# Splitting the weights of one projection three pieces ahead instead of two, in a two-layer decoder trunk

## The chip, the cores and the metric

The kernel runs on one core of one Trainium2 chip. The metric is the device time of one execution in microseconds (us). Three executions of the kernel before took 1278.33, 1278.75 and 1279.27 us, a median of 1278.75 us. The engines are named as in the profile: PE (matrix multiplication), DVE (vector), ACT (scalar), POOL, and SP, which issues the weight transfers.

## The reference

Two decoder layers over an input of 512 tokens and 1024 features, in float32. Layer 0 mixes the tokens by a gated linear recurrence, layer 1 by RWKV-7; each is followed by a gated convolutional MLP. The part that matters here is the beginning of the RWKV-7 block:

```python
xs_rkv = jnp.stack([h + xx * mix[0], h + xx * mix[1], h + xx * mix[2]])
rkv = jnp.einsum('sbtd,sde->sbte', xs_rkv, w_rkv)
r, k, v = rkv[0], rkv[1], rkv[2]
...
decay = jnp.exp(-jnp.exp(w))
...
kk = kk / jnp.maximum(jnp.linalg.norm(kk, axis=-1, keepdims=True), 1e-12)
kf = kf * (1.0 + (a - 1.0) * k_a)
...
y = _rwkv7_scan(rh, hs(decay), kh, vh, -kk, kk * ah)
```

So three products of 512x1024 by 1024x1024 (r, k, v), a normalisation of k for each head, and a recurrence over the tokens with 16 heads of 64 features. The kernel does the recurrence in chunks of 64 tokens, and needs for each chunk and head the inverse of a unit triangular matrix.

## The kernel before, in words

**Products in three matmuls.** A float32 product is made of reduced-precision ones. Each factor is split into a high part and the rest: a weight piece `raw` (128 x 1024 numbers, 512 KB) becomes `wh` by a cast on ACT (L94) and `wl` by a subtraction on DVE (L97); `mm3` (L54) then issues wh·xh, wh·xl and wl·xh. The inputs are split in the same way into pairs named `mix` or `early`, also by L94 and L97, from a tile `mt` (the token mix of one block of 128 features: L965 or L967, then L970 on DVE).

**Weight pieces.** All weights of the kernel are one list of pieces in order of use. `next_weights` asks for the piece in use: it issues the loads up to three pieces ahead and the splits up to `ahead` pieces, counted from this one and including it. Loads go through SP's queue. Raw, split and other tiles of this size share one ring of buffers.

**Projection.** `project` computes 512 output features of one of the products: four pieces of two feature blocks each (c = 0 to 3), of which the last two are used together, and four accumulators `acc`. Between its steps it calls `background`, which lets other work go on: generators in lane 0 (`rate`) and lane 1 (`rate1`), and `after`, which makes the inputs of a later product.

**Around the change.** The k product comes first, then r as two projections (features 0 to 511, then 512 to 1023), then v. In this document the pieces of the first projection of r are called pieces 1 to 4 and those of the second 5 to 8. Beside the first projection run `prepare(1)` (L1175 to L1218: decays, the norms of k, and the factors AR and BK of the recurrence for the heads 8 to 15) and `solve(0)` (L1264 on: the triangular inverses for the heads 0 to 7). `solve(0)` makes its matrices on PE (aab, L1287), copies them on ACT into D and O (L1292, L1295, L1296, in two batches of ten copies), turns D on DVE (L1300, 1.95 us in the trace), then takes 31 steps of a product and an addition on DVE, each step needing the one before (D, L1308 and X, L1310), and turns the result twice (LT, L1313 and XN, L1315). PE uses XN at L1334 (m1p). Beside the second projection, `trail(2, mv, ...)` makes the inputs `mix` of v. After v the chunk loop (pe, W, tr, tu, py and others) goes through the recurrence.

**Order.** The order of an engine's instructions is fixed when the program is built: a scheduler takes the instructions as written, with its own estimate of times, and places each engine's. At run time each engine goes through its list in that order, and an instruction that waits holds all that stand behind it on its engine.

Of the kernel before, what the change touches and what calls it, by code (L numbers as in the profile page):

```python
# [44 lines left out]
class Kernel:  # L45
# [944 lines left out]
    @staticmethod  # L990
    def bytok(t):
        return t.rearrange("p (c q t) -> p c q t", q=2, t=C)
# [135 lines left out]
    def rwkv_krv(self, pool, mk, mr, AR, BK, PC, selk, LTs):  # L1128
# [95 lines left out]
        def ev_r(b, ps):  # L1224
            self.need(("r", b))
            rr = self.outer(AR, b)
            nc.vector.tensor_tensor(rr, bytok(ps), rr, ALU.mult)

        def trail(i, out, counts):
            gen = self.mixes(i, out)  # L1230
            return lambda c: [next(gen, None) for _ in range(counts[c])]
# [3 lines left out]
        self.project(mk, lambda o, ps: nc.scalar.copy(self.outer(BK, 4 + o), bytok(ps)), after=trail(0, mr, (0, 0, 2, 2)), rate=1.2, ahead=3)  # L1235
        self.push(prepare(1))
        self.push(self.solve(0, AR, BK, LTs), 1)
        self.project(mr, lambda o, ps: ev_r(o, ps), rate=0.4, rate1=1.2)
        self.project(mr, lambda o, ps: ev_r(4 + o, ps), after=trail(2, mv, (4, 2, 2, 2)), rate=1.3, rate1=0.9)
        self.tasks[0].extend(self.tasks[1])  # L1240
        self.tasks[1].clear()
# [545 lines left out]
```

## Time and profile before

| | us |
|---|---|
| median of three runs | 1278.75 |
| profiled execution, its own time | 1279.1 |
| span of its instructions | 1277.3 |
| PE busy | 1256.0 (98%) |
| DVE busy | 929.2 (73%) |
| ACT busy | 642.8 (50%) |
| POOL busy | 131.1 (10%) |
| mean granted clock of TensorE | 0.998 |

The profiled execution is 0.35 us above the median. Its span leaves out 1.8 us around the first and last instruction. Times in the timelines are counted from the start of the span; a row has its start, its duration, the engine, the line, the operation with its output and inputs, the count of instructions drawn together, and in brackets the idle time just before it with what ended it. Durations overlap with the next instruction's, since the engines are pipelined: a PE matmul of 512 columns lasts 0.39 us in the trace, and the next starts 0.23 us later.

### The profile page before, as it was taken

The page shows a single profiled execution, that of the slowest core. Times are in us where ns is not written, and L with a number is a line of the kernel's source. Part 1 is how long each engine was busy: PE and PEld are TensorE (multiplying, and loading weights), DVE is VectorE, ACT ScalarE, POOL GpSimd, SP SyncE. Part 2 cuts the span into 40 slices and gives each one's busy share as a digit, 9 for nine tenths or more (in the row PEclk, how much of TensorE's full clock was granted, in tenths as well). Part 3 has the DMA queues.
Part 4 walks back from the last instruction along what each step waited for, and adds up shares of the span by engine and source line. Part 5 has one row for each costly group of instructions (what it writes and reads, how often), then busy time and mean ns, then how long its engine had stood idle before and what let it go on. Part 6 is the DMA issues. An engine that isn't in the chain of part 4 may idle for free. (4 is left out here: it accounts for less than half of the span.)

```text
span 1277.3 us, 22409 instructions
## 1 busy us (share of the span) xinstructions
PE 1256.0 (98%) x9259; PEld 1067.4 (84%) x9259; DVE 929.2 (73%) x1412; ACT 642.8 (50%) x1006; POOL 131.1 (10%) x206
## 2 busy tenths in 40 slices
PE   9999999999999999999999898999999999999998
PEld 8777888989898989877778797778889898989896
DVE  5998678767676767789999967778776666666654
ACT  6797455434343434559845356545644334343442
POOL 3000001010101010010012145310010101000000
PEclk9999999999999999999999999999999999999999
DMA  7312335445454544413222122122345454545431
GB/s 228 109 53 97 98 119 114 158 106 167 97 175 89 181 83 137 141 57 110 67 75 68 35 63 85 50 94 83 127 88 181 83 182 83 182 83 182 98 133 66
DMA packets 117829, 141.37 MB, mean 111 GB/s; under 512 B 10138, under 2 KB 91748, under 8 KB 117600
## 3 DMA queue, kind: packets, MB, share of 16 engines
q1 hardware_dynamic: 100528, 122.44, 29.9%
q0 software_dynamic: 16624, 16.47, 8.3%
q8 instruction: 72, 1.18, 0.4%
q10 hardware_dynamic: 576, 1.05, 0.2%
q14 instruction: 29, 0.24, 0.1%
HBM read 135.41 MB, written 4.52 MB: 110 GB/s over the span
## 5 line engine op out<-in xcount | busy, mean ns | idle before, releaser
L97 DVE TENSOR_TENSOR wl<-raw,wh 128x1024 fp32r<-128x1024 f32 (+1 forms) x161 | 194.4, 1213 | 123.6 <-ACT wh L94 103.8
L94 ACT CAST wh<-raw 128x1024 fp32r<-128x1024 f32 (+1 forms) x161 | 165.9, 1043 | 179.8 <-PE acc L54 40.7
L54 PE MATMUL accU<-xs,wh 128*128 128x512 f32 x448 | 138.6, 391 | 0.0
L54 PE MATMUL accG<-xs,wh 128*128 128x512 f32 x448 | 138.6, 390 | 0.0
L54 PE MATMUL acc<-hid,wh 128*128 128x512 f32 x384 | 117.9, 389 | 0.0
L748 DVE TENSOR_TENSOR lo<-raw,hi 128x1024 fp32r<-128x1024 f32 x70 | 85.5, 1222 | 39.4 <-PE accU L54 32.0
L747 ACT CAST hi<-raw 128x1024 fp32r<-128x1024 f32 x70 | 73.7, 1054 | 60.4 <-PE accU L54 25.3
L54 PEld LDWEIGHTS accU<-xs,wh 128*128 128x128 f32 x448 | 83.7, 188 | 17.1
L54 PEld LDWEIGHTS accG<-xs,wh 128*128 128x128 f32 x448 | 83.7, 188 | 17.0
L54 PE MATMUL accU<-xs,wl 128*128 128x512 f32 x224 | 87.2, 389 | 0.0
L54 PE MATMUL accG<-xs,wl 128*128 128x512 f32 x224 | 87.2, 389 | 0.0
L54 PE MATMUL accA<-xt,hi 128*128 128x256 f32 x480 | 83.5, 277 | 0.0
L54 PEld LDWEIGHTS acc<-hid,wh 128*128 128x128 f32 x384 | 71.4, 188 | 14.3
L54 PE MATMUL acc<-xs,wh 128*128 128x512 f32 x256 | 80.9, 398 | 0.0
L694 DVE SCALAR_TENSOR_TENSOR cv<-gpad,pv,cv 128x512 f32<-128x512 f32 x96 | 69.1, 747 | 13.1 <-ACT cv L692 12.7
L848 PE MATMUL acc<-wh,hid 128*128 128x512 f32 (+1 forms) x200 | 76.2, 381 | 0.0
L849 PE MATMUL acc<-wl,hid 128*128 128x512 f32 (+1 forms) x200 | 76.1, 381 | 0.0
L847 PE MATMUL acc<-wh,hid 128*128 128x512 f32 (+1 forms) x200 | 76.1, 381 | 0.0
L54 PE MATMUL acc<-hid,wl 128*128 128x512 f32 x192 | 74.3, 389 | 0.0
L168 POOL DMA_DIRECT2D raw<-in_ffn_w_up_dram x20 | 25.7, 1285 | 469.8 <-DVE x L863 166.5
L54 PEld LDWEIGHTS accA<-xt,hi 128*128 128x128 f32 x480 | 72.6, 188 | 0.0
L54 PE MATMUL accA<-xt,lo 128*128 128x256 f32 x240 | 66.3, 276 | 0.0
(411 smaller groups left out, 2938.0 us busy)
## 6 DMA issues: line engine op xcount, KB each, us to landing
raw<-in_ffn_w_up_dram SPq DMA_DIRECT2D x106, 512.0 KB, 3.9
raw<-in_ffn_w_down_dram SPq DMA_DIRECT2D x48, 512.0 KB, 4.0
raw<-in_ffn_w_up_dram POOLq DMA_DIRECT2D x30, 512.0 KB, 5.7
raw<-in_rwkv_w_rkv_dram SPq DMA_DIRECT2D x24, 512.0 KB, 3.8
raw<-in_lru_w_in_dram SPq DMA_DIRECT2D x16, 512.0 KB, 4.0
raw<-in_lru_w_out_dram SPq DMA_DIRECT2D x8, 512.0 KB, 3.8
raw<-in_rwkv_w_out_dram SPq DMA_DIRECT2D x8, 512.0 KB, 3.8
xd<-x SPq DMA_DIRECT2D x8, 256.0 KB, 2.1
```

The lines of the kernel that those rows point to most:

```text
L54: mm = lambda *a, **kw: self.nc.tensor.matmul(ps, *a, skip_group_check=more, **kw)
L94: put = (self.nc.vector.tensor_copy if dve else self.nc.scalar.copy)(hi, src)
L97: self.nc.vector.tensor_tensor(lo, src, hi.bitcast(F32), ALU.subtract)
L168: self.nc.gpsimd.dma_start(raw, more, accum_op=ALU.add)
L694: nc.vector.scalar_tensor_tensor(cv, pair.gp[:, e, j : j + T], cw(j), cv, ALU.mult, ALU.add)
L747: nc.scalar.copy(hi, f[p])
L748: tt(lo, f[p], hi.bitcast(F32), ALU.subtract)
L847: nc.tensor.matmul(ps, hh[:, s], wh[:, k, m], start=kk == 0, stop=False)
L848: nc.tensor.matmul(ps, hl[:, s], wh[:, k, m], start=False, stop=False)
L849: nc.tensor.matmul(ps, hh[:, s], wl[:, k, m], start=False, stop=kk == blocks - 1)
```

## The change

```diff
-        self.project(mr, lambda o, ps: ev_r(o, ps), rate=0.4, rate1=1.2)
+        self.project(mr, lambda o, ps: ev_r(o, ps), rate=0.4, rate1=1.2, ahead=3)
```

In the first projection of r each split is written one piece earlier: piece 3 in the step of piece 1, piece 4 in that of piece 2, and pieces 5 and 6 with the joined pair. The first step of the second projection has then no split left to write. No instruction is added or taken away, and SP's transfers keep their order; the scheduler places the rest anew.

On ACT the first place is the second batch of copies of `solve(0)`. Ahead of it stands fac (L1177, of `prepare(1)`). The casts `wh_5688` (before) and `wh_5605` (after) are those of piece 4, `wh_5694` (before) is that of piece 5. Before:

```order
L1177 ACTIVATE fac<-BK_4909,oka,pv 128x512
L1292 COPY D_5527<-aab 128x8x32 x2
L1295 COPY D_5527<-aab 32x8x32
L1296 COPY O<-aab 32x8x32
L1295 COPY D_5527<-aab 32x8x32
L1296 COPY O<-aab 32x8x32
L1295 COPY D_5527<-aab 32x8x32
L1296 COPY O<-aab 32x8x32
L1295 COPY D_5527<-aab 32x8x32
L1296 COPY O<-aab 32x8x32
L94 CAST wh_5688<-raw_5599 128x1024
L94 CAST wh_5694<-raw_5686 128x1024
```

and after:

```order
L1292 COPY D_5531<-aab 128x8x32
L94 CAST wh_5605<-raw_5603 128x1024
L1295 COPY D_5531<-aab 32x8x32
L1296 COPY O<-aab 32x8x32
L1295 COPY D_5531<-aab 32x8x32
L1296 COPY O<-aab 32x8x32
L1292 COPY D_5531<-aab 128x8x32
L1177 ACTIVATE fac<-BK_4909,oka,pv 128x512
L1295 COPY D_5531<-aab 32x8x32
L1296 COPY O<-aab 32x8x32
L1295 COPY D_5531<-aab 32x8x32
L1296 COPY O<-aab 32x8x32
```

The cast of piece 4 moved from behind the batch into it, and one fac with it. (The cast of piece 3 moved from behind the first batch to ahead of it.)

On DVE the same place, around the turn of D (L1300) and the first steps of the chain; `wl_5689` (before) and `wl_5606` (after) belong to piece 4, `wl_5695` to piece 5. Before:

```order
L1191 TENSOR_TENSOR AR_4907<-BK_4909,ppad_5259 128x4x128
L1300 STREAM_TRANSPOSE A<-D_5527 128x1024
L97 TENSOR_TENSOR wl_5689<-raw_5599,wh_5688 128x1024
L1308 TENSOR_TENSOR D_5527<-A,X 128x31
L1310 TENSOR_TENSOR X<-X,D_5527 128x31
L1308 TENSOR_TENSOR D_5527<-A,X 128x60
L1310 TENSOR_TENSOR X<-X,D_5527 128x30x2
L1308 TENSOR_TENSOR D_5527<-A,X 128x87
L1310 TENSOR_TENSOR X<-X,D_5527 128x29x3
L1227 TENSOR_TENSOR AR_4906<-acc_5514,AR_4906 128x4x2x64
L1308 TENSOR_TENSOR D_5527<-A,X 128x112
L97 TENSOR_TENSOR wl_5695<-raw_5686,wh_5694 128x1024
```

and after:

```order
L97 TENSOR_TENSOR wl_5606<-raw_5603,wh_5605 128x1024
L1186 TENSOR_TENSOR kp<-BK_4909,pinv 128x512
L1187 SCALAR_TENSOR_TENSOR BK_4909<-BK_4909,pv,kp 128x4x128
L1300 STREAM_TRANSPOSE A<-D_5531 128x1024
L1227 TENSOR_TENSOR AR_4906<-acc_5514,AR_4906 128x4x2x64
L1191 TENSOR_TENSOR AR_4907<-BK_4909,ppad_5259 128x4x128
L1308 TENSOR_TENSOR D_5531<-A,X 128x31
L1310 TENSOR_TENSOR X<-X,D_5531 128x31
L1308 TENSOR_TENSOR D_5531<-A,X 128x60
L1310 TENSOR_TENSOR X<-X,D_5531 128x30x2
L1308 TENSOR_TENSOR D_5531<-A,X 128x87
L1227 TENSOR_TENSOR AR_4906<-acc_5515,AR_4906 128x4x2x64
```

The subtraction of piece 4 moved from behind the turn to ahead of it, and L1191 the other way. Further on the steps of the chain stand more often directly behind each other (12 neighbours of the chain with nothing between them, up to the place shown next, where before had 5).

The second place on DVE is where the last inputs of v and the last piece of r (piece 8, `wl_5955` and `wh_5954` in both) meet. Before:

```order
L1310 TENSOR_TENSOR X<-X,D_5527 128x16x16
L1218 SCALAR_TENSOR_TENSOR AR_4907<-AR_4907,nkk,knb 128x4x128
L1308 TENSOR_TENSOR D_5527<-A,X 128x255
L970 SCALAR_TENSOR_TENSOR mt<-x,pv,mt 128x511
L1310 TENSOR_TENSOR X<-X,D_5527 128x15x17
L1218 SCALAR_TENSOR_TENSOR AR_4907<-AR_4907,nkk,knb 128x4x128
L1308 TENSOR_TENSOR D_5527<-A,X 128x252
L97 TENSOR_TENSOR mix<-mt,mix 128x512
L1310 TENSOR_TENSOR X<-X,D_5527 128x14x18
L97 TENSOR_TENSOR wl_5955<-raw_5874,wh_5954 128x1024
```

and after:

```order
L1310 TENSOR_TENSOR X<-X,D_5531 128x15x17
L97 TENSOR_TENSOR mix<-mt,mix 128x512
L1218 SCALAR_TENSOR_TENSOR AR_4907<-AR_4907,nkk,knb 128x4x128 x2
L1308 TENSOR_TENSOR D_5531<-A,X 128x252
L965 TENSOR_SCALAR mt<-x,om 128x512
L1310 TENSOR_TENSOR X<-X,D_5531 128x14x18
L970 SCALAR_TENSOR_TENSOR mt<-x,pv,mt 128x511
L1218 SCALAR_TENSOR_TENSOR AR_4907<-AR_4907,nkk,knb 128x4x128 x2
L97 TENSOR_TENSOR mix<-mt,mix 128x512
L97 TENSOR_TENSOR wl_5955<-raw_5874,wh_5954 128x1024
```

The L970 whose `mt` is cast just ahead of piece 8 now stands behind three more instructions of the chain: X 15x17, D 252 and X 14x18.

On ACT at that place the cast of piece 8 stands directly behind the cast of that `mt`. Before:

```order
L1210 CAST rec<-rec 40x512
L94 CAST mix<-mt 128x512
L1368 COPY decay<-PC 64x8x8 x4
L94 CAST mix<-mt 128x512
L94 CAST wh_5954<-raw_5874 128x1024
L94 CAST wh_5960<-raw_5952 128x1024
```

and after:

```order
L1210 CAST rec<-rec 40x512
L1368 COPY decay<-PC 64x8x8 x3
L94 CAST mix<-mt 128x512
L1368 COPY decay<-PC 64x8x8
L94 CAST mix<-mt 128x512
L94 CAST wh_5954<-raw_5874 128x1024
L94 CAST wh_5960<-raw_5952 128x1024
```

One cast of `mix` changed places with three small copies; the cast of piece 8 stays behind the second one.

## The prediction

> **What bounds the kernel now.** I read the busy times first, then PE's waits, then the stretch of the change in its timelines.
>
> ```profile
> PE 1256.0 (98%) x9259; PEld 1067.4 (84%) x9259; DVE 929.2 (73%) x1412; ACT 642.8 (50%) x1006; POOL 131.1 (10%) x206
> PEclk9999999999999999999999999999999999999999
> ```
>
> PE is busy for 1256.0 of 1277.3 us, nearly all of it at full clock. The edit leaves every matmul in place, so it can change only PE's waits and its clock. The waits of PE from 640 to 740 us, with total, count and longest:
>
> ```profile
> PE pe L1468 <- DVE tu L1513: 1.8, 2, 1.1
> PE acc L54 <- ACT wh L94: 1.6, 1, 1.6
> PE tr L1438 <- DVE W L1431: 1.5, 1, 1.5
> PE m1p L1334 <- DVE XN L1315: 0.7, 1, 0.7
> ```
>
> The second row is the wait that the edit bears on. In PE's timeline, with the rows to which I return:
>
> ```profile
> 634.36 0.69 PE L1287 MATMUL aab<-AR,BK 64*64 64x64 f32 x32
> ...
> 640.93 1.21 PE L54 MATMUL acc<-mix,wh 128*128 128x512 f32 x4 [1.57 <-ACT wh L94]
> ...
> 670.89 0.39 PE L54 MATMUL acc<-mix,wl 128*128 128x512 f32 x1
> 671.12 2.07 PE L54 MATMUL acc<-mix,wh 128*128 128x512 f32 x8
> ...
> 695.12 1.20 PE L1334 MATMUL m1p<-XN,O 32*32 32x32 f32 x64 [0.75 <-DVE XN L1315]
> ...
> 719.36 0.68 PE L1468 MATMUL pe<-tu,W 128*64 128x64 f32 x14 [1.09 <-DVE tu L1513]
> ```
>
> PE waits 1.57 us for piece 4. Piece 8 (the row at 671.12) starts without a wait. ACT shows why piece 4 is late:
>
> ```profile
> 635.28 0.82 ACT L1177 ACTIVATE fac<-BK,oka,pv 128x512 f32<-128x512 f32 x1 [1.38 <-DVE BK L1192]
> 636.12 0.65 ACT L1292 COPY D<-aab 128x256 f32<-128x256 f32 x2
> ...
> 639.06 0.37 ACT L1295 COPY D<-aab 32x256 f32<-32x256 f32 x1
> 639.45 0.36 ACT L1296 COPY O<-aab 32x256 f32<-32x256 f32 x1
> 639.84 2.95 ACT L94 CAST wh<-raw 128x1024 fp32r<-128x1024 f32 x3
> ...
> 669.45 0.62 ACT L94 CAST mix<-mt 128x512 fp32r<-128x512 f32 x1 [4.26 <-DVE mt L970]
> 669.98 2.00 ACT L94 CAST wh<-raw 128x1024 fp32r<-128x1024 f32 x2
> ```
>
> Its cast begins at 639.84, behind ten copies. The last two rows are the other place: piece 8's cast begins at 669.98 behind a cast of mix that waited 4.26 us for DVE's mt, and ends about 671.0, just as PE arrives. That cover is nearly zero. DVE is the engine with no slack here; the row of windows from 639.4 to 695 us gives PE, PEld, DVE, ACT and POOL busy:
>
> ```profile
> 639.40:695.00 55.60, 53.44 (x418) 43.33 (x418) 54.75 (x114) 25.30 (x50) 7.08 (x18) 1.00 0.23 71
> ```
>
> DVE is busy for 54.75 of 55.60 us. Whatever is put ahead of an instruction there delays it in full.
>
> **The change part by part.**
>
> *The wait for piece 4.* In the new order its cast follows the batch's first copy. The last aab ends at 634.36 + 0.69 = 635.05, a copy takes half of 0.65, a cast a third of 2.95 (0.98): cast done at about 636.4. PE arrives at 640.93 - 1.57 = 639.36. The wait goes: -1.57 on PE. Pieces 5 and 6 follow directly and are wanted only from 650 us, so they cost nothing.
>
> *The turn of D.* The batch took from 636.12 to 639.43 = 3.31, until its last D. Now it can begin at 635.10, but has a cast (0.98) and a fac (0.82, of which 0.72 until the next) inside: 635.10 + 3.31 + 0.98 + 0.72 = 640.11. DVE's rows:
>
> ```profile
> 638.42 0.68 DVE L1191 TENSOR_TENSOR AR<-BK,ppad 128x512 f32<-128x512 f32 x1
> 639.46 1.95 DVE L1300 STREAM_TRANSPOSE A<-D 128x1024 f32<-128x1024 f32 x1 [0.35 <-ACT D L1295]
> 641.35 1.17 DVE L97 TENSOR_TENSOR wl<-raw,wh 128x1024 fp32r<-128x1024 f32 x1
> 642.45 0.19 DVE L1308 TENSOR_TENSOR D<-A,X 128x31 f32<-128x31 f32 x1
> 642.67 0.21 DVE L1310 TENSOR_TENSOR X<-X,D 128x31 f32<-128x31 f32 x1
> ...
> 644.48 0.27 DVE L1308 TENSOR_TENSOR D<-A,X 128x112 f32<-128x112 f32 x1
> 644.66 1.22 DVE L97 TENSOR_TENSOR wl<-raw,wh 128x1024 fp32r<-128x1024 f32 x1
> ...
> 668.68 0.74 DVE L970 SCALAR_TENSOR_TENSOR mt<-x,pv,mt 128x511 f32<-128x511 f32 x1
> 669.34 0.41 DVE L1310 TENSOR_TENSOR X<-X,D 128x255 f32<-128x255 f32 x1
> ...
> 670.33 0.41 DVE L1308 TENSOR_TENSOR D<-A,X 128x252 f32<-128x252 f32 x1
> ```
>
> The turn started at 639.46, 0.03 after its last copy; it will start at about 640.14, so +0.7. DVE itself is there by 639.11 + 1.1 - 0.6 = 639.6 (it takes on a subtraction and gives L1191 away), so ACT sets it.
>
> *DVE up to the last mt before piece 8 (L970 at 668.68).* Start of the turn +0.7; the subtraction of piece 4 leaves, -1.1 (641.35 to 642.45); L1191 comes, +0.6; X 15x17, D 252 and X 14x18 come ahead, about 0.33 each, +1.0. Then the neighbours. D at 642.45 ends at 642.64 and the X that needs it starts at 642.67, 0.03 later; D at 644.48 ends at 644.75 and the independent subtraction starts at 644.66, 0.09 earlier. A dependent neighbour so costs about 0.11 more than an unrelated one, and there are 12 where there were 5: +0.8. Sum 0.7 - 1.1 + 0.6 + 1.0 + 0.8 = +2.0. The transposes rec and knb of `prepare(1)` stand later on PE; at most some 0.4 of waiting for them comes on DVE, the far bound being zero: I take 0.2, so +2.2. Bounds: with no price on neighbours +1.2; with everything late together +2.6.
>
> *The new wait.* The mt, mix, and piece 8's cast hang together on ACT, so the cast and PE's start on piece 8 move from 671.12 to about 673.3. PE would be there at 671.12 - 1.57 = 669.55. So a wait of 3.3 to 3.7 us stands at piece 8, of which 0.4 may already be taken at piece 7, whose subtraction also stands behind more of the chain. PE is 2.2 late where it had been 1.57 early.
>
> *From there to the chunks.* XN's end moves by +0.7 - 1.1 + 0.6 and 8 more dependent neighbours in all (0.9), +1.1, to +1.8 if all small waits add. m1p had 0.75 of wait, so PE's lateness of 2.2 shrinks to max(2.2 - 0.75, 1.1 to 1.8), about 1.7. The masks W and the first tu stand two steps of the chain later: the wait of 1.09 at 719.36 grows by up to 1.4, and the 1.5 at tr, which waits for W, gives most back. I take +0.3 (bounds -0.3 and +0.8). Together +2.0.
>
> *The clock.* This is the largest doubt. The windows show one place in this part where the clock was lowered (the column ahead of the DMA share is the granted clock; PE busy is the second number), and two stretches with waits where it was not:
>
> ```profile
> 793.00:794.00 1.00, 0.33 (x3) 0.20 (x4) 1.00 (x3) 0.69 (x2) 0.43 (x1) 1.00 0.95 393
> 794.00:795.00 1.00, 0.00 (x0) 0.00 (x0) 0.01 (x1) 0.00 (x0) 1.00 (x1) 1.00 0.47 197
> 795.00:796.00 1.00, 0.79 (x27) 0.79 (x28) 0.17 (x1) 0.00 (x0) 0.89 (x3) 1.00 0.08 33
> 796.00:797.00 1.00, 0.41 (x14) 0.31 (x9) 0.99 (x3) 0.69 (x2) 0.40 (x1) 0.91 0.00 0
> 797.00:798.00 1.00, 1.00 (x20) 0.88 (x23) 0.97 (x2) 0.04 (x1) 0.00 (x0) 0.50 0.06 16
> ...
> 800.00:801.00 1.00, 1.00 (x7) 0.91 (x7) 1.00 (x2) 0.26 (x1) 0.00 (x0) 0.88 0.69 110
> ...
> 638.00:642.00 4.00, 2.43 (x12) 1.66 (x11) 3.65 (x5) 3.92 (x8) 0.00 (x0) 1.00 0.46 131
> 730.00:735.00 5.00, 3.50 (x69) 2.53 (x62) 4.79 (x10) 1.60 (x4) 1.38 (x2) 1.00 0.00 0
> ```
>
> In 793 to 797 PE was busy for 1.53 of 4 us; then the clock stood at 0.50 from about 796.8 to 800.2, 3.4 us. At 638 to 642 it was busy for 2.43 of 4 and the clock stayed. A wait of 3.3 us or more at piece 8 leaves 0.7 of 4 us busy, below the closed case; but the stretch that counts may be cut at another point, and a wait split in two halves lies nearer the open case. I hold a closing likelier than not, 2 to 1. At half clock 3.4 us of matmuls do 1.7 us of work, less what of it falls into the wait: 1.1 to 1.7, of which the rest of the wait at m1p takes some 0.1. So about +1.3.
>
> The Trainium skill (TensorE: Matmul & The Clock Gate, Part 1: The HAM clock gate) says that the clock falls to half after at least one idle window of about 3.4 us, on windows that run freely. The length of the slow stretch agrees (3.4 us at 0.50). A gap of 3.3 to 3.7 us seldom fills such a window whole, so by that rule the clock would stay and the sum would be +2.0; the trace speaks against the strict reading, since it closed with 1.53 of 4 us busy.
>
> *Sum.* +2.0 + 1.3 = +3.3 on the profiled execution, 1279.1 to 1282.4; that execution is 0.35 above the median of 1278.75, so about 1282.0 as a median.
>
> **The rivals.** A change under 0.2% (2.6 us) is about what a measurement of this kernel cannot tell from none: from 1276.2 to 1281.3.
>
> *The new wait comes, the clock stays.* For it: two stretches with 30 to 40% idle kept their clock. Against it: the one at 794. Time: 1278.75 + 2.0 = 1280.8, no measurable change. It decides itself by how much of the wait falls into one stretch of about 3.4 us.
>
> *The delay on DVE is mostly absorbed.* If the dependent neighbours cost nothing (-0.8) and the copies of the batch begin early enough for the turn to keep its time (-0.7), mt is late by 0.7 and PE waits about 2.2 at piece 8, for a net of 0.7; m1p's 0.75 takes that, and what is left is -0.3 to +0.8: 1278.5 to 1279.6. This ends on the other side: not slower. The point from which it decides is an mt late by less than about 1.2. Against it: the 0.03 and 0.09 above, and ACT's order.
>
> *The gain stays.* If no new wait appears at piece 8, PE keeps its 1.57: 1277.2. That needs mt no later than before, against +1.0 from the three chain steps alone. Even this is under 0.2%.
>
> **How the numbers follow.** New wait with the slow clock 0.50 (1282.0, its own range 1281.2 to 1283.2), new wait alone 0.25 (1280.8), absorbed 0.17 (1279.0), gain kept 0.08 (1277.2). The predicted time is that of the first, rounded to 1281.9 since the smaller end of the clock's price is as likely as the larger. Slower by over 0.2%: nearly all of the first, with a little of the second, 0.48. Faster: 1277.2 is inside the band, so 0.03 only. The same: 0.49. The range from 1278.9 to 1283.0 leaves out the gain, half of the absorbed case and the far end of the first, about 0.19.
>
> **What the changed profile would show.** PE's row "acc <- ACT wh 1.6" at 641 gone, and a new wait of 3 us or more at the first wh row of piece 8, near 670 to 673 us; the turn L1300 at about 640.1; the last mt near 670.9; m1p's wait below 0.75; the granted clock at 0.50 for 3.4 us near 674 to 677 us. I am wrong if that wait is under 2 us, or if the clock row reads 1.00 there.

## The result, and the profile after

The changed kernel takes 1281.23 us (median of 20 runs, 1280.16 to 1282.74), the kernel before 1278.61 us on the same chip (20 runs, 1277.40 to 1279.87). The ratio is 1.0022, with a 95% interval from 1.0016 to 1.0028: 2.6 us slower. That is just about the 0.2% that I had named as the limit of what can be told from no change, but with 20 runs of each the interval lies clear of 1, so the kernel did become slower. The profiled execution took 1282.44 us (span 1280.4), so it lies 1.2 us above its median. Two of the twelve executions of e6_p4, below, took 1382.30 and 1996.60 us at a mean granted clock of 0.85 and 0.58, and its figures leave these two out.

The page's rows on the engines and the granted clock:

```profile
PE 1258.0 (98%) x9259; PEld 1069.4 (84%) x9259; DVE 930.4 (73%) x1412; ACT 642.7 (50%) x1006; POOL 130.6 (10%) x206
PEclk9999999999999999999998999999999999999999
```

The work is the same, and one slice of the clock now reads 8. PE's waits from 640 to 740 us:

```profile
PE acc L54 <- ACT wh L94: 3.3, 1, 3.3
PE pe L1468 <- DVE tu L1513: 2.9, 2, 2.0
PE acc L54 <- DVE wl L97: 0.8, 1, 0.8
PE tr L1438 <- DVE W L1431: 0.4, 1, 0.4
```

The wait on wh is still one wait, but of 3.3 us instead of 1.6, and the wait of m1p for XN has left the list. PE's timeline says which piece it is:

```profile
617.91 0.60 PE L1208 MATMUL rec<-ident,n 128*40 128x128 f32 x4 [0.49 <-DVE n L1204]
...
663.99 0.50 PE L54 MATMUL acc<-mix,wl 128*128 128x512 f32 x1 [0.75 <-DVE wl L97]
...
670.48 0.40 PE L54 MATMUL acc<-mix,wl 128*128 128x512 f32 x1
674.14 3.78 PE L54 MATMUL acc<-mix,wh 128*128 128x512 f32 x8 [3.27 <-ACT wh L94]
...
699.22 1.20 PE L1334 MATMUL m1p<-XN,O 32*32 32x32 f32 x64
```

The first row serves to set the two traces against each other. In the trace of before it starts at 617.00, and XN, to which I return, at 692.89:

```profile
617.00 0.60 PE L1208 MATMUL rec<-ident,n 128*40 128x128 f32 x4 [0.50 <-DVE n L1204]
```

```profile
692.89 2.08 DVE L1315 STREAM_TRANSPOSE XN<-X 128x1024 f32<-128x1024 f32 x1
```

The row rec stands ahead of everything that the edit moves, so the second trace is 0.91 us late from its start; that has to be taken off each time below. Where I compare the experiments' traces too, I count from this row in each (617.58 in e1, 617.25 in e2, 617.63 in e3, 617.82 in e5, 617.91 in e6, 617.41 in e7, 617.03 in e11, 618.08 in e12). The wait for piece 4 is gone. Piece 8 waits 3.27 us, and its first eight matmuls take 3.78 us where they took 2.07. The windows show why they are slow (PE busy is the second number, the granted clock the one before the DMA share):

```profile
670.00:671.00 1.00, 0.88 (x4) 0.38 (x2) 1.00 (x3) 0.00 (x0) 0.91 (x4) 1.00 0.96 340
671.00:672.00 1.00, 0.00 (x0) 0.00 (x0) 1.00 (x3) 0.00 (x0) 0.86 (x3) 1.00 0.96 291
672.00:673.00 1.00, 0.00 (x0) 0.00 (x0) 1.00 (x2) 0.47 (x1) 0.00 (x0) 0.70 0.61 209
673.00:674.00 1.00, 0.00 (x0) 0.00 (x0) 1.00 (x3) 1.00 (x3) 0.00 (x0) 0.50 0.10 35
...
678.00:679.00 1.00, 1.00 (x3) 0.71 (x3) 0.39 (x1) 0.00 (x0) 0.00 (x0) 0.50 0.42 142
679.00:680.00 1.00, 1.00 (x5) 0.86 (x4) 0.46 (x1) 0.00 (x0) 0.00 (x0) 0.89 0.00 0
```

The clock falls to 0.50 at about 672.4, in the middle of the wait, and comes back at about 679.2: 6.8 us, of which PE spends 5.1 us (674.14 to 679.2) on matmuls at half speed. The median execution probably loses less. The 20 executions have a mean clock from 0.995 to 0.998, with the median between 0.996 and 0.997, and the profiled one is among the four with the lowest. A stretch of 3.4 us at half clock lowers the mean by 1.7 / 1280 = 0.0013, so by this estimate the median execution has about one such stretch fewer; which one is not on record.

ACT and DVE show what came late:

```profile
640.74 0.36 ACT L1295 COPY D<-aab 32x256 f32<-32x256 f32 x1
...
672.52 0.62 ACT L94 CAST mix<-mt 128x512 fp32r<-128x512 f32 x1 [3.81 <-DVE mt L970]
673.05 1.99 ACT L94 CAST wh<-raw 128x1024 fp32r<-128x1024 f32 x2
```

```profile
641.14 2.12 DVE L1300 STREAM_TRANSPOSE A<-D 128x1024 f32<-128x1024 f32 x1 [0.39 <-ACT D L1295]
...
671.72 0.77 DVE L970 SCALAR_TENSOR_TENSOR mt<-x,pv,mt 128x511 f32<-128x511 f32 x1
...
679.54 0.69 DVE L1227 TENSOR_TENSOR AR<-acc,AR 128x512 f32<-128x512 f32 x1 [1.16 <-PE acc L54]
...
696.87 2.14 DVE L1315 STREAM_TRANSPOSE XN<-X 128x1024 f32<-128x1024 f32 x1
```

The turn of D starts when the last D copy ends, the cast of piece 8 stands behind a cast of mix that waited for DVE's mt, and the row at 679.54 is new: DVE itself waits 1.16 us for PE, whose accumulators the slow clock has made late.

### The profile page after: what moved, and what is told of

The parts are those of the page before. It is cut to its first block, busy times and chain, and to the rows that moved or that the text cites. A ratio compares the mean times of both kernels' runs of the same rounds, so it can differ in the third digit from the quotient of the medians.

```text
span 1280.4 us, 22404 instructions
## 1 busy us (share of the span) xinstructions
PE 1258.0 (98%) x9259; PEld 1069.4 (84%) x9259; DVE 930.4 (73%) x1412; ACT 642.7 (50%) x1006; POOL 130.6 (10%) x206
```

## The experiments

All were run in five rounds beside the kernel before. My theory was that the loss has two parts, a late mt that opens a wait at piece 8 and the clock that this wait lowers. The rivals were that the clock costs nothing in the end, and that the cast inside ACT's batch is the whole cause.

**Filling the wait (e1_fill10).** Ten matmuls of a zero weight onto the accumulator; in the trace they stand directly ahead of piece 8. (The tile `zero` and the parameter `fill` are added too.) The scheduler placed a few others anew: ACT's four small copies `decay` now stand behind piece 8's cast, one weight transfer goes out ahead of the transfer `lnw` (L1390) instead of behind it, and the mt of piece 8 starts 53.48 us after rec instead of 53.81.

```diff
-                    for k in range(1 if first else 0, kc):
+                    for k in [self.nc.tensor.matmul(pss[o], self.zero, xs[x0][0], start=False, stop=False) for _ in range(fill if c == n - 1 and o == nob - 1 else 0)][:0] or range(1 if first else 0, kc):
...
-self.project(mr, ..., rate=1.3, rate1=0.9)
+self.project(mr, ..., rate=1.3, rate1=0.9, fill=10)
```

> The changed kernel with ten more matmuls of a zero weight (128x128 by 512 columns, adding zeros to acc) on PE directly ahead of the first matmul of piece 8, where PE waits 3.27 us in the profile of the changed kernel; order on ACT, DVE and POOL as in the changed kernel. They take ten times 0.23 = 2.3 us and should fit into the wait. Theory (part of the loss is the clock, lowered because PE is idle there): the wait at piece 8 shrinks to about 1.0 us, the granted clock reads 1.00 from 660 to 690 us, and the time falls by 0.5 to 1.2 to 1280.0 to 1280.7, about 1.5 to 2.0 above before. Rival (the clock costs nothing in the end, the delay alone makes the loss): 1281.2, as the changed kernel. Rival (PE's throughput after the wait matters, the wait was not free): 1283.5.

Measured: 1279.16 us, 2.1 below the changed kernel, ratio to before 1.0007 (0.9999 to 1.0016). Its timeline, and its row of windows beside that of the changed kernel below it:

```profile
670.39 2.45 PE L214 MATMUL acc<-early,zero 128*128 128x512 f32 x10
673.46 2.14 PE L54 MATMUL acc<-mix,wh 128*128 128x512 f32 x8 [0.62 <-ACT wh L94]
...
697.00 1.20 PE L1334 MATMUL m1p<-XN,O 32*32 32x32 f32 x64 [0.76 <-DVE XN L1315]
```

```profile
640.00:690.00 50.00, 48.62 (x327) 39.05 (x326) 48.98 (x103) 20.77 (x39) 7.76 (x15) 1.00 0.21 68
```

```profile
640.00:690.00 50.00, 45.98 (x277) 36.34 (x276) 47.76 (x97) 18.05 (x31) 5.11 (x15) 0.93 0.20 68
```

PE does 2.3 us more work and the kernel is 2.1 us faster. The clock stays at 1.00, and the eight matmuls of piece 8 take 2.14 us again. The gain is larger than the 0.5 to 1.2 that I expected. Counted from rec, piece 8 starts after 55.88 us, in the changed kernel after 56.23; m1p (697.00) starts after 79.42, in the changed kernel after 81.31. So of the 1.9 us that lie between the two at m1p, 1.5 arise behind the start of piece 8, where the one runs at full clock and the other at half.

One thing stood in the way of that reading. Among PE's waits of the changed kernel, over the whole run, stands

```profile
PE pd L1506 <- issue: 1.4, 1, 1.4
```

and it was gone in this profile, perhaps because ten more instructions stand ahead of it. The 1.9 us stand ahead of that place and can't come from it, but the time of the whole kernel can. So three controls follow.

**The same number of instructions without the work (e11_tiny10).** The ten matmuls at the same place in the changed kernel, 16 columns wide instead of 512.

```diff
-self.nc.tensor.matmul(pss[o], self.zero, xs[x0][0], start=False, stop=False)
+self.nc.tensor.matmul(pss[o][:, 0:16], self.zero, xs[x0][0][:, 0:16], start=False, stop=False)
```

> The ten zero matmuls of the first experiment at the same place in the changed kernel, but 16 columns wide instead of 512: as many instructions on PE, hardly any work (an estimate of 0.05 us each from the 64-column matmuls of the chunk loop), so PE stays idle there. It separates two readings of the first experiment, in whose profile the wait 'issue' of 1.4 us at L1506 near 798 us was gone as well. Theory (the clock): the wait at piece 8 stays near 2.8 us or more, the clock is lowered there in most runs, and the time is 1280.4 to 1281.4, near the changed kernel's. Rival (ten more instructions move the place of the 'issue' wait, and that was the gain): the 'issue' wait gone, 1279.2 to 1279.9.

Measured: 1281.21 us, ratio to before 1.0027 (1.0016 to 1.0039): the changed kernel's time, as expected. The "issue" wait was gone in this profile too, so its absence alone does not give the time of the first experiment.

```profile
669.84 1.18 PE L214 MATMUL acc<-early,zero 128*128 128x16 f32 x10
673.78 3.43 PE L54 MATMUL acc<-mix,wh 128*128 128x512 f32 x8 [2.76 <-ACT wh L94]
```

```profile
669.80:673.20 3.40, 1.22 (x11) 1.08 (x10) 3.15 (x7) 2.01 (x6) 1.79 (x7) 1.00 0.26 37
673.20:676.60 3.40, 2.82 (x7) 2.24 (x8) 3.15 (x6) 0.53 (x1) 3.22 (x7) 0.51 0.96 262
```

PE waits 2.76 us, the clock goes to 0.50 in the next 3.4 us, and the eight matmuls take 3.43 us. So ten matmuls that leave PE idle do not keep the clock up, and ten that fill the wait do. The difference in time, 1281.21 - 1279.16 = 2.05 us, is not the price of the clock alone. Between the two programs stands only the width of ten matmuls, but the scheduler placed other engines' instructions differently:

```profile
671.13 1.01 ACT L1368 COPY decay<-PC 64x64 f32<-64x64 f32 x4 [4.11 <-PE acc L214]
...
677.46 1.05 ACT L94 CAST wh<-raw 128x1024 fp32r<-128x1024 f32 x1 [3.74 <-DMA raw<-in_rwkv_w_rkv_dram]
```

```profile
678.54 1.23 DVE L97 TENSOR_TENSOR wl<-raw,wh 128x1024 fp32r<-128x1024 f32 x1 [1.73 <-ACT wh L94]
```

The four copies wait for the zero matmuls and stand ahead of the casts of mix and of piece 8, so piece 8 starts 56.75 us after rec, 0.87 later than in e1, before any matmul of piece 8 is slow. And DVE waits 1.73 us for a cast whose weight transfer stands behind `lnw` on SP's queue, which went out at 671.16; in e1 one such transfer went out ahead of it, at 662.10. The cleaner figure for the clock is the 1.5 us above.

**The zero matmuls in the kernel before (e5_before_fill10 and e12_before_tiny10).** The same edits with `ahead` left at 2, wide and narrow. The narrow ones stand directly ahead of piece 8 in the trace, the wide ones in three groups from 671.94 to 678.29 among its matmuls.

```diff
-self.project(mr, lambda o, ps: ev_r(o, ps), rate=0.4, rate1=1.2, ahead=3)
+self.project(mr, lambda o, ps: ev_r(o, ps), rate=0.4, rate1=1.2)
```

> Control for the ten zero matmuls: the same ten in the kernel before, at the same place (beside piece 8, where PE does not wait there). Theory (they helped the changed kernel only by keeping PE busy in a long wait): here they cost what the later waits do not take up, 2.3 us less the 0.75 at m1p and some at the chunk loop, so 0.8 to 1.6 above before: 1279.5 to 1280.3. Rival (the matmuls help by themselves, or moved something else): no slower than before, 1278.7 or less.

> The same ten narrow matmuls in the kernel before. Theory (they cost at most 0.5 us of PE, and moving the 'issue' wait is worth little in most runs): 1278.4 to 1279.0. Rival (moving the 'issue' wait is worth 1.0 to 1.9): 1277.0 to 1277.9, faster than before.

Measured: wide 1279.16 us, ratio 1.0002 (0.9994 to 1.0011), less than expected; narrow 1279.72 us, ratio 1.0012 (1.0003 to 1.0021), more than expected. Neither is shown to be faster than before, so nothing says that the ten instructions help by themselves. At m1p PE is 0.82 us later than before in the wide one's profile and 0.97 in the narrow one's, counted from rec; the "issue" wait is gone in both, and what that is worth in the median is open. So is why the narrow ones cost more than the wide ones: they take 1.0 us of PE, not the 0.5 that I had estimated, and the runs spread from 1277.9 to 1282.4.

**The two halves (e2_p34 and e3_p56).** Only pieces 3 and 4, or only 5 and 6, split a step earlier.

```diff
-ws = [self.next_weights(1 if first else ahead) for _ in cs]
+ws = [self.next_weights(1 if first else ahead if isinstance(ahead, int) else ahead[c]) for c in cs]
...
+e2_p34: ahead=[3, 3, 2, 2]
+e3_p56: ahead=[2, 2, 3, 3]
```

> Half of the change: only pieces 3 and 4 split a step earlier, 5 to 8 as before. ACT's second batch of copies has the cast of piece 4 and a fac inside, as in the changed kernel. Theory (the delay of the last mt is made of the late turn of D, +0.7, and of the chain steps and neighbours that the early splits of pieces 5 and 6 bring): the wait for piece 4 (1.6) is gone, a wait of 1.5 to 2 us stands at piece 8, the clock mostly stays, +0.5 to +0.9 on before: 1279.1 to 1279.6. Rival (the cast inside ACT's batch is the whole cause): a wait of 3 us at piece 8 and the full +2.6. Rival (nothing but the early cast of piece 4 matters): -1.6.

> The other half: only pieces 5 and 6 split a step earlier, 3 and 4 as before. Theory: the wait for piece 4 stays at 1.6, a wait of about 1.5 us appears at piece 8, since more steps of the chain stand ahead of its mt, and the time is 1.0 to 1.6 above before: 1279.7 to 1280.3. Rival (the cast inside ACT's batch is the whole cause): no wait at piece 8 and no difference to before. Rival (the two halves do not add): the full +2.6.

Measured: e2 1278.92 us, ratio 1.0003 (0.9994 to 1.0011), a little below what I expected; e3 1279.83 us, ratio 1.0010 (1.0001 to 1.0018), as expected. The waits for wh, first of e2, then of e3:

```profile
671.64 2.14 PE L54 MATMUL acc<-mix,wh 128*128 128x512 f32 x8 [1.74 <-ACT wh L94]
```

```profile
641.55 1.21 PE L54 MATMUL acc<-mix,wh 128*128 128x512 f32 x4 [1.56 <-ACT wh L94]
...
673.02 2.11 PE L54 MATMUL acc<-mix,wh 128*128 128x512 f32 x8 [1.48 <-ACT wh L94]
```

Each half makes its own wait at piece 8, 1.74 and 1.48 us, and the whole change has 3.27 (with 0.75 at piece 7 before it). A wait is not yet a delay, though. Counted from rec, piece 8 starts 0.27 us later than before in e2, 1.27 in e3 and 2.11 in the whole: the wait of e2 is nearly all PE coming earlier, which costs nothing, and that of e3 is nearly all the late mt. The times go with these delays, 0.2 and 1.1 us by the medians. The whole costs 2.6, with 0.6 us more delay than the two halves together and the slow clock besides; in both halves' profiles the eight matmuls of piece 8 take 2.1 us, at full clock. So the cast in ACT's batch is not the whole cause, and two waits at which the clock stayed became one that lowered it.

**Piece 8 ahead of mix (e4_both3_1).** Pieces 7 and 8 also split earlier.

```diff
-self.project(mr, ..., rate=1.3, rate1=0.9)
+self.project(mr, ..., rate=1.3, rate1=0.9, ahead=[2, 3, 3, 3])
```

> The changed kernel with pieces 7 and 8 also split earlier (three ahead from the second step of the second projection of r), so that the cast of piece 8 stands ahead of the cast of mix on ACT. Theory (DVE is full from 640 to 695 us and sets the pace; the place at which PE meets it is secondary): no wait at piece 8, but a wait of about 2 us at the first piece of v for its subtraction on DVE, and m1p waits 1.7; about +1.8 on before, 1280.4, with the clock mostly at 1.00. Rival (the order on ACT behind the late mt is the cause): no wait of over 0.7 us from 650 to 690 us, and 1.6 faster than before, 1277.0.

Measured: 1282.05 us, ratio 1.0033 (1.0021 to 1.0046). PE's waits there:

```profile
678.65 0.39 PE L1258 MATMUL acc<-wl,mix 128*128 128x256 f32 x1 [1.95 <-DVE wl L97]
...
697.03 1.20 PE L1334 MATMUL m1p<-XN,O 32*32 32x32 f32 x64 [1.97 <-DVE XN L1315]
```

```profile
695.00:698.40 3.40, 1.43 (x67) 1.35 (x67) 3.40 (x3) 1.54 (x3) 3.03 (x4) 0.99 0.26 86
698.40:701.80 3.40, 3.40 (x48) 3.18 (x49) 1.45 (x3) 1.15 (x2) 3.15 (x3) 0.50 0.26 73
```

The wait at piece 8 is gone and stands at the next piece, for DVE's subtraction, and at m1p, both as expected. The time was missed by 1.7 us: I had expected the clock to stay, and it fell in this profile after the wait at m1p. That this makes up the 1.7 us is not shown.

**Piece 4 alone (e6_p4).** `ahead=[2, 3, 2, 2]`.

> Only piece 4 split a step earlier; 3, 5, 6, 7 and 8 as before. Theory (removing the wait for piece 4 gains 1.57 at its place, and DVE, full until XN, hands it to a later wait): the wait for piece 4 is gone, rec waits about 1.4 us instead of 0, m1p waits 0.7 to 0.9, and the time is that of before, 1278.5 to 1279.0. Rival (the gain stays when 5 and 6 are left alone): 1277.1.

Measured: 1278.81 us (ten executions), ratio 1.0000 (0.9991 to 1.0009), as expected. The wait for piece 4 is gone, and by the medians nothing is gained:

```profile
PE rec L1208 <- DVE n L1204: 1.1, 1, 1.1
PE m1p L1334 <- DVE XN L1315: 0.7, 1, 0.7
PE sst L1200 <- ACT tmp L1196: 0.3, 1, 0.3
```

rec waits 1.06 and sst 0.32 of the 1.57 us that PE comes earlier. In this profile m1p still starts 0.5 us earlier than before, counted from the first rec; the medians can't tell that from nothing.

**Fewer chain steps ahead of the mt (e7_r2_rate07).** The changed kernel with `rate1=0.7` instead of 0.9 in the second projection.

> The changed kernel with rate1=0.7 instead of 0.9 in the second projection of r, so fewer steps of the chain stand ahead of the last mt before piece 8. Theory (the chain steps ahead of that mt make it late, and the clock goes with the length of the wait): the wait at piece 8 falls from 3.3 to about 2.0 us, the clock is lowered there seldom or for one stretch only, and the time is 0.8 to 1.3 above before: 1279.5 to 1280.0. Rival (ACT's batch and the turn set it): the wait stays at 3 us and the time at 1281.2.

Measured: 1279.71 us, ratio 1.0011 (1.0002 to 1.0019), as expected. The steps of the chain bear on the mt: it starts 52.27 us after rec instead of 53.81, and the wait at piece 8 is shorter:

```profile
672.08 2.11 PE L54 MATMUL acc<-mix,wh 128*128 128x512 f32 x8 [1.85 <-ACT wh L94]
```

The steps that are put off come later: XN starts 80.89 us after rec instead of 78.96, and m1p waits 1.38 us for it.

**Versions meant to be faster (e8_p3_rate07_t3, e9_p3_rate07_t3_again, e10_p34_rate07_t3).** `rate1=0.7` and `trail(2, mv, (3, 2, 2, 2))`, with piece 3 alone early (`ahead=[3, 2, 2, 2]`) or pieces 3 and 4 (`[3, 3, 2, 2]`).

> A version meant to keep the gain: only piece 3 split a step earlier, rate1=0.7 in the second projection of r, and one mix of v fewer after its first step (3, 2, 2, 2). Theory: no wait of over 0.5 us from 625 to 690 us (neither piece 4 nor piece 8), m1p waits about 0.8 as before, and 0.8 to 1.3 faster than before: 1277.4 to 1277.9. Rival (DVE's load until XN gives every gain back before m1p): 1278.7.

> The version of the run before again (piece 3 alone split a step earlier, rate1=0.7 and 3, 2, 2, 2 in the second projection of r), for a narrower interval: it was 0.9 us below before by the medians, with an interval from 0.9987 to 1.0004. Theory: 0.6 to 1.1 below before again, 1277.6 to 1278.1. Rival (chance): within 0.3 of before.

> The same with piece 4 split earlier too. Theory (once fewer chain steps stand ahead of the last mt, the early split of piece 4 no longer makes a wait at piece 8): rec waits about 0.6, the wait at piece 8 is below 0.3 where the half with pieces 3 and 4 alone had 1.7, m1p waits about 0.8, and the time is 0.5 to 1.1 below before: 1277.6 to 1278.2. Rival (the late turn of D holds piece 8 up in any case): a wait of 1.5 at piece 8 and 1278.9.

Measured: the first 1277.86 us, ratio 0.9995 (0.9987 to 1.0004), and again 1278.73 us, 1.0001 (0.9992 to 1.0010); the second 1278.47 us, 1.0001 (0.9992 to 1.0010). The first gain did not come again. Their profiles have no wait at piece 8, and neither is shown to be faster than before. The waits of e10:

```profile
PE m1p L1334 <- DVE XN L1315: 1.5, 1, 1.5
PE rec L1208 <- DVE n L1204: 1.2, 2, 0.7
```

m1p takes 1.5 us, twice what it took before and what I had expected (1.7 in both profiles of the other version): what is gained ahead of it is mostly given back there. In e10's profile the clock also falls to 0.50 behind this wait, from 701.2 to 704.6. Both are faster than the changed kernel by over 2 us.

## Why the prediction was right

The mechanism came as predicted up to the slow clock (times of after less 0.91):

- The turn of D: predicted at 640.14, came at 641.14 - 0.91 = 640.23.
- The last mt: predicted +2.2, came at 671.72 - 0.91 = 670.81 against 668.68, +2.1. The chain has the larger share in it. In e2 the turn is 0.76 late and the mt 0.26, since the subtraction of piece 4 has left, as the sum had it; in e3 the turn is on time and the mt 1.27 late; in e7 fewer steps of the chain take 1.5 off.
- Piece 8: predicted at 673.3 with a wait of 3.3 to 3.7 us, came at 674.14 - 0.91 = 673.23 with 3.27, and 0.75 at piece 7, where I had up to 0.4.
- The clock: 0.50 as predicted, but for 6.8 us in the profiled run instead of 3.4. Wherever the clock is low in a profile, away from the end of the kernel, it is so for 3.4 or 6.8 us, so it seems to be set by stretches of 3.4 us. The wait lay across the border of two of them at 672.4, with PE busy for 1.88 and 1.66 of 3.40 us (the rows are in the last section).

Of the two terms of the sum, the clock came out nearly as predicted, partly by luck, and the delay was put too high.

- *The clock* was +1.3. From the start of piece 8 to that of m1p the changed kernel takes 25.08 us and e1 23.54, so 1.5. Behind this stand two deviations. The profile has two slow stretches where I had one, and PE loses 2.3 us of work in them. And m1p takes up 0.76 of that, the wait that it has in e1 and not in the changed kernel, where I had 0.1.
- *From there to the chunks* was +2.0 for the delay alone. In e1, with the clock kept up, m1p starts 1.30 us later than before and the row of pe ahead of the "issue" wait (791.43, before 789.59) 1.26 later. So this term is too large by 0.7: XN comes 1.29 late, near the lower end of my 1.1 to 1.8, where I had taken 1.7; and the chunk loop adds nothing, where I had +0.3. There the first wait for tu grew by 0.9 and that for W shrank by 1.0.

In the profile of after XN starts 3.1 late (696.87 - 0.91 = 695.96 against 692.89), beyond my 1.8, because DVE waited for PE's slow matmuls (the row at 679.54). That cost little, since PE itself comes as late as XN.

Together that is 3.1 in the profile of after at the row of pe ahead of the "issue" wait (793.62), against 3.3 predicted. Two things stand outside the sum. Behind that row the profile of after gets about 1 us back: the last matmul (1273.85, before 1270.79) is 2.15 late. Some of it is the "issue" wait, 1.44 us instead of 1.73, and the wait for tu just behind it, 0.20 instead of 0.58; the rest I did not trace. And the profiled execution came at 1282.44 where I had 1282.4, but that is luck: 0.91 us of it arose ahead of the change. The median of 1281.23 lies 0.7 below the 1281.9 that I gave.

The rival with the clock staying (1280.8) lies nearer to the median, but the granted clock of 0.50 at the wait decides against it, and e1 shows that keeping it up pays. The rival of an absorbed delay fell on the wait of 3.27, that of a kept gain on the same row; by the medians even piece 4 alone (e6) keeps none of its 1.57.

Against the Trainium skill (TensorE: Matmul & The Clock Gate, Part 1: The HAM clock gate): its windows of about 3.4 us that run freely agree with the slow stretches of 3.4 and 6.8 us here. Its rule that the clock falls after at least one idle window is too strict if a wholly idle one is meant: in e11 PE was busy for 1.22 of the 3.40 us ahead of the fall.

## What to carry to other kernels

A wait that is taken away from the engine that bounds the kernel is a gain only if the engine that feeds it has slack up to the next place where they meet; here DVE was busy for 54.75 of 55.60 us, and PE's gain went into later waits. Ask of a new wait what it is made of: where the engine only comes earlier it costs nothing, where its input comes later it does. And add up the waits that a change brings together in one place: two of 1.7 and 1.5 us cost 0.2 and 1.1 us when they stood alone, and 2.6 us as one of 3.3, in good part because the clock then fell. Where such a wait can't be avoided, useless matmuls in it can be cheaper than idling: 2.3 us of them made this kernel 2.1 us faster. Last, a control that differs in one place of the program can still differ in the order of other engines, as e11 did, so read its trace before its time.

## What the runs showed of the hardware that I had not expected

The clock falls after stretches that are far from wholly idle, and the share of idle time alone does not decide it. It fell after 3.4 us with PE busy for 1.43 of 3.40 (e4, the row at 695.00 above), and did not after 1.56 of 3.40 in e3, whose next stretch is at 1.00:

```profile
719.40:722.80 3.40, 1.56 (x62) 1.49 (x62) 3.30 (x7) 0.37 (x1) 1.00 (x2) 1.00 0.00 0
722.80:726.20 3.40, 3.40 (x71) 3.00 (x62) 3.23 (x8) 1.12 (x3) 0.58 (x2) 1.00 0.03 7
```

In the changed kernel it fell after a stretch with more work than either:

```profile
669.00:672.40 3.40, 1.88 (x8) 0.94 (x6) 3.37 (x7) 0.00 (x0) 2.67 (x9) 1.00 0.88 292
672.40:675.80 3.40, 1.66 (x4) 1.37 (x5) 3.40 (x7) 2.51 (x3) 0.00 (x0) 0.50 0.10 36
```

PE was busy for 1.88 of 3.40 us there, and what it ran were matmuls of 512 columns, where e3's stretch held 62 small ones.

The length of the wait does not decide it either, since it matters how the wait lies to the borders of the stretches. In e5 PE waited 2.71 us (until 722.52) and the clock stayed; in e11 it waited 2.03 us (until 723.91) and the clock fell. The wait of e5 lay across a border (counted back in steps of 3.413 us from the next fall, at 1274.14), that of e11 within one stretch, first e5, then e11:

```profile
717.77:721.18 3.41, 2.04 (x17) 1.70 (x15) 3.38 (x8) 0.36 (x1) 0.00 (x0) 1.00 0.00 0
721.18:724.59 3.41, 2.07 (x65) 1.94 (x66) 3.27 (x7) 0.37 (x1) 0.96 (x2) 1.00 0.03 7
```

```profile
721.03:724.45 3.42, 1.39 (x21) 1.12 (x20) 3.39 (x7) 0.00 (x0) 0.81 (x2) 1.00 0.00 0
724.45:727.86 3.41, 3.41 (x58) 3.15 (x54) 3.17 (x9) 0.37 (x1) 0.19 (x1) 0.50 0.03 7
```

Away from the end of the kernel, all falls came after stretches with PE busy for 1.1 us (before, ending at 796.82) to 2.0 us (e6, ending at 795.15) of 3.4, and of the stretches that kept the clock the idlest is that of e3. What the gate counts besides busy time is left open.

Ten matmuls of 16 columns took 1.0 us of PE (672.24 to 673.27 in e12), 0.10 each, about twice my estimate from the 64-column ones of the chunk loop.
